# Branch C's output projection as seven block products in a hybrid encoder trunk

## The chip, the cores and the metric

The kernel runs on one core of a Trainium2 chip. The metric is the device time of one execution in microseconds. Engines are named as the profile names them: PE (matmuls) with PEld (its weight loads), DVE and ACT (vector and scalar work), POOL, and SP, which only issues DMAs here. L12 is line 12 of the kernel before.

## The reference

Two layers of an encoder trunk over 512 positions of 1024 channels, all in float32. Per layer:

```python
xn = rms_norm(x, ln1[l])
z = xn @ w_in[l]                       # all branches' columns and the gates gz
y_a = rms_norm(o_a, a_norm[l]) * silu(a_g)         # o_a: gated linear scans, 4 heads
y_b = spatial_gating(gelu(b_u), gelu(b_v), w_s[l], b_s[l])
y_c = window_attention(qh, kh, vh, sink[l])        # 512 x 512
gates = sigmoid(gz.reshape(bsz, s_len, 3, D_MODEL))
merged = (gates[:, :, 0] * (y_a @ w_br[l, 0])
          + gates[:, :, 1] * (y_b @ w_br[l, 1])
          + gates[:, :, 2] * (y_c @ w_br[l, 2]))   # each w_br: 512 x 1024
x = x + merged @ w_out[l]
hn = rms_norm(x, ln2[l])
x = x + square(relu(hn @ w_up[l])) @ w_down[l]
```

A final rms_norm follows. The change touches the last term of `merged`, a product of 512 x 512 by 512 x 1024 in each layer, and the place of some norm work at the start of layer 0.

## The kernel before, in words

**Precision and matmul form.** Every float32 operand of a large product is split into a high and a low part (fp32r): ACT casts the high part, DVE subtracts it from the original to get the low part (`split`, L255, for activations; `wsplit`, L201, for weights, 128 x 1024 at a time). A product of two such pairs takes three matmuls: high by high, low by high, high by low. A weight chunk is loaded by SP (512 KB) into one of two buffers `wr` (`wload`, L179); its parts lie in one of three buffers `wh` and `wl`.

**Block products.** Several large products already go through `seven` (L422). A product is cut into 2 x 2 blocks on each side and computed as seven block products in place of eight, from sums of blocks: `left_sums` (L375) makes the sums of the left operand (differences of 256 columns, then splits of 512), and in `seven` DVE adds the weight blocks in place before products 6, 5 and 4. The order of products is 1, 2, 6, 7, 5, 4, 3. Products 1, 6, 5 and 3 accumulate in the same two PSUM banks, and so do 7 and 4, so each result is read out by a callback `on` before the next product of that chain adds to it: P1, P2 (added to P1's result), P16, P7, P165, P74, P1653. Weight splits, weight sums and callbacks are traced with raised priority (`hp`, L124).

**Order of the work.** The program is traced in Python and a scheduler puts each engine's instructions into an order by priority, against its own model of time; on the chip each engine runs its queue in that order. `later(n)` lowers the priority of what it holds, `behind(mark)` binds instructions of one engine behind another instruction.

**Layer, stage by stage.** From the norm (`n1`: split tiles `xs` in 16 slots with the tag "x") come first three units of `seven`, u = 0 to 2, K = 1024 (24 matmuls for each block product): u = 0 the values of branches A and B (`on_tok`), u = 1 and 2 the gates of branches C and A (`on_gate`), which are passed through tanh and written to DRAM (`thd`). In layer 0 the norm's reciprocal root `rc` is late, so `on_tok` works unscaled. After product 7 of unit 0 comes `norm_rows` (L347): four matmuls against the identity (eight in the trace) spread `rc` over rows (`bc`, L285), ACT copies them to `rb`. After the unit, L896 to L898 scale the eight tiles vt and bv by `rc` on ACT. DVE's three small scalings of `rc` (L835 to L837) stand ahead of unit 0.

Then heads of branch A's scan (`a_head`, L617), branch B, branch C's attention (`c_run`, L1096) and projections are traced with priorities that let them interleave. Branch C's output comes as four tiles `yc`, 128 features by 512 positions each; the last, yc[3], comes from the transposes at L1067, the products `po` at L1078 and a copy at L1080. At L1125 the output gates of branch A (`gate_a`, four projections `ag`) are traced, and behind them **branch C's projection**, L1128 to L1137: the four yc are split, and for each half fl of the 1024 output channels `proj_tok` (L236) runs two weight chunks of two k-tiles each, for four blocks of 128 positions, into four PSUM banks (m, m, c, c). DVE multiplies each bank by its gate plus one (L1136) into `mC`, eight tiles in the slots "x". The gates come back from DRAM by POOL (`gates`, L1082) into seven slots "ch". Branch A's gates (`tha`) are loaded into "x" as well. Branch A's projection `yA` follows (L1165), is gated (L1168) and added (L1169), the sum is transposed (`mT`, L1153), and `wo` follows.

Of the kernel before, what the change touches and what calls it, by code (L numbers as in the profile page):

```python
# [6 lines left out]
F32 = mybir.dt.float32  # L7
# [5 lines left out]
P = 128  # L13
# [46 lines left out]
def trunk(tc, xT, xt, ws, vec, fnb, bsb, snk, wst, rope, cmask, amask, ident, out):  # L60
# [26 lines left out]
    part = {}  # L87
    BANKS = {"m": 2, "a": 2, "c": 2, "s": 2}
    PAIRS, AHEAD = ((), (2,), (2,), (2,)), ((), (1,), (1,), (1,))
    GROUPS = (("m", "m", "c", "c"), ("a", "a", "s", "s"))  # L90
    WR, WB, NZ, NSM, NQ = 2, 3, 2, 3, 8

# [254 lines left out]
    def norm_rows(n):  # L347

        pt = bcast(n.rc)
        n.rb = T("rb", "rb")  # L350
        nc.scalar.copy(n.rb, pt)
# [20 lines left out]
        h.update({2: two(v_, 0), 4: two(v_, 1)})  # L372
        return left_sums(new, h, u, v, sb_, held)

    def left_sums(new, h, u, v, sb_=None, held=False):  # L375
        V = nc.vector
        a11, a21, a12, a22 = u[:, 0:HT], u[:, HT:], v[:, 0:HT], v[:, HT:]
        if sb_ is None:
            sb_ = part["wq"].tile([P, 2, HT], F32, tag="sf", bufs=2, name=nm("sf"))
            V.tensor_tensor(sb_[:, 0], a11, a21, ALU.subtract)  # L380
        sa = part["wq"].tile([P, 2, HT], F32, tag="sf", bufs=2, name=nm("sf"))
        V.tensor_tensor(sa[:, 0], a22, a21, ALU.subtract)
        V.scalar_tensor_tensor(sa[:, 1], sa[:, 0], -1.0, a11, ALU.mult, ALU.subtract)
# [12 lines left out]
        if not held:  # L396
            first(new)
        V.scalar_tensor_tensor(sb_[:, 1], a12, -1.0, sa[:, 1], ALU.mult, ALU.subtract)
        if held:
            return first, second  # L400
        second(new)
# [20 lines left out]
    def seven(raw, hs, name, on, order=(1, 2, 6, 7, 5, 4, 3), between=None, after=1, apart=False, swap=False):  # L422

        b11, t3, b22, b21 = raw
        V = nc.vector

        banks = {}
        use = {1: ("c", b11, "P1"), 2: ("m", b21, "P2"), 6: ("c", b11, "P16"), 7: ("a", t3, "P7"),
               5: ("c", t3, "P165"), 4: ("a", b21, "P74"), 3: ("c", b22, "P1653")}

        def mms(pt, p, k, xh, xl, hi, lo, c, start):
            t = slice(p * P, (p + 1) * P)
            nc.tensor.matmul(pt, xh[:, t], hi[:, c], start=start and k == 0, stop=False, skip_group_check=True)  # L433
            nc.tensor.matmul(pt, xl[:, t], hi[:, c], start=False, stop=False, skip_group_check=True)  # L434
            nc.tensor.matmul(pt, xh[:, t], lo[:, c], start=False, stop=k == 3, skip_group_check=True)  # L435

        for n in order:
            tag, w, which = use[n]
            bank = {"c": "a", "a": "c"}.get(tag, tag) if swap else tag
            start = n in (1, 2, 7)  # L440
            if start:
                banks[tag] = [PT(bank, name + {"c": "A", "m": "B", "a": "C"}[tag]) for _ in range(2)]
            pts = banks[tag]
            with hp():
                for i in range(2):
                    if n == 6:
                        V.tensor_tensor(b11[i], b11[i], t3[i], ALU.add)
                    elif n == 5:
                        V.tensor_tensor(t3[i], b11[i], b22[i], ALU.subtract)
# [3 lines left out]
            for s_ in range(2):  # L453
                with hp():
                    split_w.append(wsplit(w[s_]))
                if not apart or n != order[-1]:
                    for k2 in range(2):
                        c = slice(k2 * S, (k2 + 1) * S)
                        for p in range(2):
                            mms(pts[p], p, 2 * s_ + k2, *hs[2 * s_ + k2][n], *split_w[s_], c, start)  # L460
# [325 lines left out]
    for l in range(DEPTH):  # L786
# [25 lines left out]
        def project_bu():  # L812
            pts = proj_four(xs, "bu", l, "bu", banks="mmcc" if l else "mmaa")
            if l == 0:
                raw = [T("l2", "bu") for _ in pts]
                for t, pt in zip(raw, pts):
                    nc.scalar.copy(t, pt)
                return raw
            norm_rows(n1)
            return [evac(pt, "l2", "bu") for pt in pts]  # L820
# [40 lines left out]
                bv[p] = T("tv", "bv")  # L861
                A.activation(bv[p], pt, AF.Copy, scale=nlo)

        past = []

        def on_gate(i):
            w = {}

            def keep(z, t, fl):
                nc.gpsimd.dma_start(thd[:, i * 4 + t, fl * S:(fl + 1) * S], z)  # L870

            def on(which, p, pt):
                A, V = nc.scalar, nc.vector
                if which in ("P1", "P16", "P7"):
                    w[which, p] = T("zt", "zt")
                    A.copy(w[which, p], pt)
# [12 lines left out]
        for u in range(3):  # L889
            nxt = uload(l, "un", u + 1) if u < 2 else None  # L890
            if u == 0:
                if l:
                    seven(raw, hx, "t", on_tok, (1, 7, 6, 2, 5, 4, 3), lambda: bu.extend(project_bu()), swap=(u + l) % 2)
                else:
                    seven(raw, hx, "t", on_tok, (1, 2, 6, 7, 5, 4, 3), lambda: norm_rows(n1), 7, swap=(u + l) % 2)
                    for t in vt + bv:  # L896
                        i = (vt + bv).index(t) % 4
                        nc.scalar.activation(t, t, AF.Copy, scale=rc[:, i:i + 1])  # L898
# [339 lines left out]
        for qd in range(4):  # L1238
# [30 lines left out]
                    if f == 3:  # L1269
                        early_sums(raw, mark)  # L1270

            def between():
# [141 lines left out]
```

## Time and profile before

| | us |
|---|---|
| median of 3 runs (1647.73 to 1648.71) | 1648.09 |
| profiled execution | 1647.19 |
| its span, first to last instruction | 1645.4 |
| branch C's projection, layer 0: first and last matmul start | 392.93 and 426.26 |
| the same, layer 1, last | 1243.3 |

The profile is of one execution. A row of a timeline has the start in us, the duration, engine, line, operation, output and inputs with their shapes; in brackets stands how long the engine was idle before it and what ended that. Matmuls are pipelined: a 512-column matmul is shown with 0.39 us, while the next one starts earlier. A row of the groups has the count, the busy time, the mean in ns and the idle time before. A row of stretches has the length and the busy time of each engine in that stretch.

### The profile page before, as it was taken

The numbers are of one execution on the slowest core, as the hardware profiler recorded it, in microseconds if no ns is written. First come the engines' busy times: TensorE is split into PE (matmuls) and PEld (weight loads), VectorE is DVE, ScalarE is ACT, GpSimd is POOL, SyncE is SP. The second block draws the span as 40 slices with busy tenths as digits, with TensorE's granted clock in tenths as the row PEclk, the third lists the DMA queues.
The fourth block names the chain that finished last, engine by engine and source line by source line (L and its number), as shares of the span: only waits on it lengthen the run. The fifth ranks groups of instructions, "written<-read, shape, count | busy, mean of one in ns | idle before, by whom it ended". The sixth has DMA issues, their size and how long they took to land.

```text
span 1645.4 us, 24316 instructions
## 1 busy us (share of the span) xinstructions
PE 1631.2 (99%) x9137; PEld 1376.4 (84%) x9137; DVE 1359.1 (83%) x2183; ACT 1013.8 (62%) x1731; POOL 102.9 (6%) x165
## 2 busy tenths in 40 slices
PE   9999999999999999999999999999999999999997
PEld 7788888888888898989888888888888888989896
DVE  7888979677758988888989869887877589898987
ACT  7667567677247564646666655886862464647374
POOL 0012000000300000000010110000003000000001
PEclk9999999999999999999999999999999999999999
DMA  8343221322625233232423432222226343232411
GB/s 309 103 153 125 77 90 72 103 97 84 237 90 192 99 107 103 103 107 98 141 90 125 145 121 77 77 84 103 97 78 243 108 162 119 87 128 77 129 65 52
DMA packets 55590, 191.55 MB, mean 116 GB/s; under 512 B 7376, under 2 KB 7632, under 8 KB 55472
## 3 DMA queue, kind: packets, MB, share of 16 engines
q1 hardware_dynamic: 44352, 154.43, 27.4%
q0 software_dynamic: 10688, 35.00, 5.7%
q8 instruction: 72, 1.18, 0.3%
q10 hardware_dynamic: 432, 0.55, 0.1%
q14 instruction: 46, 0.38, 0.1%
HBM read 173.18 MB, written 16.78 MB: 115 GB/s over the span
## 4 chain that ended last, share of the span: by engine, by line
PE 91%; ACT 3%; DVE 3%; DMA 2%; issue 1%; POOL 0%; SPq 0%; POOLq 0%; DVEq 0%; ACTq 0%
PE up L208 4%; PE up L209 4%; PE up L210 4%; PE dA L434 4%; PE dA L433 4%; PE dA L435 4%; PE us L522 2%; PE us L524 2%; PE us L523 2%; PE f L210 2%; PE f L209 2%; PE wo L252 2%; PE wo L250 2%; PE f L208 2%; PE wo L251 2%; PE dC L434 2%
## 5 line engine op out<-in xcount | busy, mean ns | idle before, releaser
L203 ACT CAST wh<-wq 128x1024 fp32r<-128x1024 f32 x214 | 225.3, 1053 | 206.2 <-PE dA L434 56.4
L204 DVE TENSOR_TENSOR wl<-wq,wh 128x1024 fp32r<-128x1024 f32 x214 | 259.9, 1219 | 66.5 <-ACT wh L203 64.4
L203 ACT CAST wh<-wr 128x1024 fp32r<-128x1024 f32 x164 | 172.0, 1049 | 156.4 <-PE wo L251 27.1
L204 DVE TENSOR_TENSOR wl<-wr,wh 128x1024 fp32r<-128x1024 f32 x164 | 199.9, 1219 | 62.3 <-ACT wh L203 56.1
L210 PE MATMUL up<-xh,wl 128*128 128x512 f32 x320 | 124.7, 390 | 0.0
L209 PE MATMUL up<-xl,wh 128*128 128x512 f32 x320 | 124.7, 390 | 0.0
L208 PE MATMUL up<-xh,wh 128*128 128x512 f32 x320 | 124.4, 391 | 0.0
L434 PE MATMUL dA<-wh,sh 128*128 128x512 f32 x256 | 99.7, 389 | 0.0
L433 PE MATMUL dA<-wh,sh 128*128 128x512 f32 x256 | 98.4, 389 | 0.0
L435 PE MATMUL dA<-wl,sh 128*128 128x512 f32 x256 | 91.8, 389 | 0.0
L656 DVE TENSOR_TENSOR ex<-ex 128x512 f32<-128x512 f32 x112 | 74.8, 685 | 3.4 <-ACT kt L647 3.2
L210 PEld LDWEIGHTS up<-xh,wl 128*128 128x128 f32 x320 | 60.1, 188 | 12.4
L208 PEld LDWEIGHTS up<-xh,wh 128*128 128x128 f32 x320 | 60.1, 188 | 12.2
L209 PEld LDWEIGHTS up<-xl,wh 128*128 128x128 f32 x320 | 60.1, 188 | 12.2
L644 ACT ACTIVATE qt<-ex 128x512 f32<-128x512 f32 x56 | 37.9, 677 | 31.4 <-DVE ex L656 29.8
L435 PEld LDWEIGHTS dA<-wl,sh 128*128 128x128 f32 x256 | 48.1, 188 | 10.0
L433 PEld LDWEIGHTS dA<-wh,sh 128*128 128x128 f32 x256 | 48.0, 188 | 10.0
L434 PEld LDWEIGHTS dA<-wh,sh 128*128 128x128 f32 x256 | 48.0, 188 | 9.9
L523 PE MATMUL us<-xs,wh 128*128 128x256 f32 x192 | 54.0, 283 | 0.0
L522 PE MATMUL us<-xs,wh 128*128 128x256 f32 x192 | 54.0, 283 | 0.0
L524 PE MATMUL us<-xs,wl 128*128 128x256 f32 x192 | 53.3, 283 | 0.0
L208 PE MATMUL gz<-xh,wh 128*128 128x512 f32 x128 | 51.0, 399 | 0.7 <-DVE gz L792 0.7
(438 smaller groups left out, 4775.7 us busy)
## 6 DMA issues: line engine op xcount, KB each, us to landing
wr<-in_ws_dram SPq DMA_DIRECT2D x158, 512.0 KB, 3.5
wq<-in_ws_dram SPq DMA_DIRECT2D x124, 512.0 KB, 4.3
thd<-zt POOLq DMA_DIRECT2D x32, 256.0 KB, 2.6
gt<-thd POOLq DMA_DIRECT2D x32, 256.0 KB, 4.3
mgd<-mg POOLq DMA_DIRECT2D x16, 256.0 KB, 2.6
mB<-mgd POOLq DMA_DIRECT2D x16, 256.0 KB, 6.6
x<-in_xT_dram SPq DMA_DIRECT2D x8, 256.0 KB, 7.7
xt<-in_xt_dram SPq DMA_DIRECT2D x8, 256.0 KB, 7.9
```

Of the source, the lines that this page charges most:

```text
L203: nc.scalar.copy(hi, raw)
L204: nc.vector.tensor_tensor(lo, raw, hi.bitcast(F32), ALU.subtract)
L208: nc.tensor.matmul(pt, whi, xhi, start=first, stop=False)
L209: nc.tensor.matmul(pt, whi, xlo, start=False, stop=False)
L210: nc.tensor.matmul(pt, wlo, xhi, start=False, stop=last)
L433: nc.tensor.matmul(pt, xh[:, t], hi[:, c], start=start and k == 0, stop=False, skip_group_check=True)
L434: nc.tensor.matmul(pt, xl[:, t], hi[:, c], start=False, stop=False, skip_group_check=True)
L435: nc.tensor.matmul(pt, xh[:, t], lo[:, c], start=False, stop=k == 3, skip_group_check=True)
L522: nc.tensor.matmul(pt, hi[:, c], xh, start=n in (1, 2, 7) and k == 0, stop=False, skip_group_check=True)
L523: nc.tensor.matmul(pt, hi[:, c], xl, start=False, stop=False, skip_group_check=True)
L524: nc.tensor.matmul(pt, lo[:, c], xh, start=False, stop=k == 3, skip_group_check=True)
L656: nc.vector.tensor_tensor(o_ap, o_ap, ap_of(ex, i_, [[istep, 2]] + z), ALU.add)
```

## The change

Branch C's projection goes through `seven`. Four weight chunks are loaded at once, the first two into the `wr` buffers, the others into two buffers of the tag "z2". The left blocks are made from yc[k] and yc[k + 2], k = 0 and 1, by `left_sums`, whose temporaries and sums now lie in the slots "x". Product 1 needs yc[0] and yc[1], product 2 needs yc[2] and yc[3], the other five need sums of all four. Each product has 12 matmuls. Products 7 and 4 use the banks "s" (which the attention uses too), the others c and m. `on_yc` evicts P1, P16, P7 and P1653 on ACT, adds the others on DVE from PSUM into the same tiles, and gates each finished tile on DVE. The eight gates of branch C are asked for in the order in which the tiles are finished.

In layer 0 the norm broadcast moves from behind product 7 of unit 0 to behind product 1 of unit 1, and the eight scalings to behind the first ACT copy of unit 1.

`seven` becomes general in the number of weight tiles and k-tiles, takes the bank map as an argument, and hands its `between` the last matmul of the first product; for the other users this leaves the work as it was. The diff without those lines:

```diff
-    def left_sums(new, h, u, v, sb_=None, held=False):
+    def left_sums(new, h, u, v, sb_=None, held=False, sf=None):
...
-        sa = part["wq"].tile([P, 2, HT], F32, tag="sf", bufs=2, name=nm("sf"))
+        sa = sf() if sf else part["wq"].tile([P, 2, HT], F32, tag="sf", bufs=2, name=nm("sf"))
...
-            if n == after and between:
-                between()
+            if n == order[0] and between:
+                between(end_)
...
+        def rows_behind(mark):
+            with behind(mark):
+                norm_rows(n1)
+
-        past = []
+        past, kept = [], []
...
-                    A.copy(w[which, p], pt)
+                    kept.append(A.copy(w[which, p], pt))
...
-                    seven(raw, hx, "t", on_tok, (1, 2, 6, 7, 5, 4, 3), lambda: norm_rows(n1), 7, swap=(u + l) % 2)
-                    for t in vt + bv:
-                        i = (vt + bv).index(t) % 4
-                        nc.scalar.activation(t, t, AF.Copy, scale=rc[:, i:i + 1])
+                    seven(raw, hx, "t", on_tok, (1, 2, 6, 7, 5, 4, 3), swap=TURN if (u + l) % 2 else None)
             else:
-                seven(raw, hx, "g", on_gate(u - 1), swap=(u + l) % 2)
+                seven(raw, hx, "g", on_gate(u - 1), between=None if l or u > 1 else rows_behind, swap=TURN if (u + l) % 2 else None)
+                if l == 0 and u == 1:
+                    with behind(kept[0]):
+                        for ts in (vt, bv):
+                            for i, t in enumerate(ts):
+                                nc.scalar.activation(t, t, AF.Copy, scale=rc[:, i:i + 1])
...
-            ys = y_split(yc, "yh")
-            mcs = []
-            for fl in range(2):
-                th = gates("ch", 0, fl)
-                pts = proj_tok(ys, "yC", (l, "y", 2, fl), 0)
-                mcs.append([T("x", "mC") for _ in range(4)])
-                for t in range(4):
-                    with hp():
-                        nc.vector.scalar_tensor_tensor(mcs[fl][t], th[t], 1.0, pts[t], ALU.add, ALU.mult)
+            raw = []
+            for i, (kh, fl) in enumerate(((0, 0), (0, 1), (1, 1), (1, 0))):
+                with hp():
+                    t = Z2("wb").rearrange("p a b -> p (a b)") if i > 1 else sb.tile([P, CW], F32, tag="wr", bufs=WR, name=nm("wr"))
+                    nc.sync.dma_start(t, ws[CHUNK[(l, "y", 2, fl, kh)]])
+                raw.append([t])
+            early_sums(raw)
+            hy = []
+            for k in range(2):
+                u, v = yc[k], yc[k + 2]
+                p1 = T("yh", "yh", F32R).rearrange("p (a b) -> p a b", a=2)
+                split(u[:, 0:HT], p1[:, 0], p1[:, 1])
+                v_ = (T("yh", "yh", F32R), T("yh", "yl", F32R))
+                split(v, *v_)
+                h = {1: (p1[:, 0], p1[:, 1]), 2: two(v_, 0), 4: two(v_, 1)}
+                left_sums(lambda: T("x", "ysum", F32R), h, u, v, sf=lambda: T("x", "sf").rearrange("p (a b) -> p a b", a=2))
+                hy.append(h)
+            mcs = [[None] * 4, [None] * 4]
+            th = {}
+            for fl, t in ((0, 0), (0, 1), (1, 2), (1, 3), (0, 2), (0, 3), (1, 0), (1, 1)):
+                th[fl, t] = T("ch", "gt")
+                nc.gpsimd.dma_start(th[fl, t], thd[:, t, fl * S:(fl + 1) * S])
+
+            def on_yc(which, p, pt):
+                A, V = nc.scalar, nc.vector
+                t, fl = {"P1": (p, 0), "P2": (p, 0), "P16": (2 + p, 0), "P74": (2 + p, 0), "P7": (2 + p, 1), "P165": (2 + p, 1), "P1653": (p, 1)}[which]
+                if which in ("P1", "P16", "P7", "P1653"):
+                    mcs[fl][t] = T("x", "mC")
+                    A.activation(mcs[fl][t], pt, AF.Copy, scale=-1.0 if fl else 1.0)
+                else:
+                    V.tensor_tensor(mcs[fl][t], mcs[fl][t], pt, ALU.subtract if fl else ALU.add)
+                if which in ("P2", "P165", "P74", "P1653"):
+                    V.scalar_tensor_tensor(mcs[fl][t], th[fl, t], 1.0, mcs[fl][t], ALU.add, ALU.mult)
+
+            seven(raw, hy, "v", on_yc, swap={"a": "s"})
```

More of the change, by code (lines that the diff above doesn't have):

```diff
@@ L89, in trunk @@
     PAIRS, AHEAD = ((), (2,), (2,), (2,)), ((), (1,), (1,), (1,))
+    TURN = {"c": "a", "a": "c"}
     GROUPS = (("m", "m", "c", "c"), ("a", "a", "s", "s"))
@@ L378, in left_sums @@
         if sb_ is None:
-            sb_ = part["wq"].tile([P, 2, HT], F32, tag="sf", bufs=2, name=nm("sf"))
+            sb_ = sf() if sf else part["wq"].tile([P, 2, HT], F32, tag="sf", bufs=2, name=nm("sf"))
             V.tensor_tensor(sb_[:, 0], a11, a21, ALU.subtract)
-        sa = part["wq"].tile([P, 2, HT], F32, tag="sf", bufs=2, name=nm("sf"))
+        sa = sf() if sf else part["wq"].tile([P, 2, HT], F32, tag="sf", bufs=2, name=nm("sf"))
         V.tensor_tensor(sa[:, 0], a22, a21, ALU.subtract)
@@ L420, in early_sums, with seven @@
                 nc.vector.tensor_tensor(b12, b12, b22, ALU.add)
-    def seven(raw, hs, name, on, order=(1, 2, 6, 7, 5, 4, 3), between=None, after=1, apart=False, swap=False):
+    def seven(raw, hs, name, on, order=(1, 2, 6, 7, 5, 4, 3), between=None, apart=False, swap=False):
         b11, t3, b22, b21 = raw
@@ L434, in mms @@
             nc.tensor.matmul(pt, xl[:, t], hi[:, c], start=False, stop=False, skip_group_check=True)
-            nc.tensor.matmul(pt, xh[:, t], lo[:, c], start=False, stop=k == 3, skip_group_check=True)
+            return nc.tensor.matmul(pt, xh[:, t], lo[:, c], start=False, stop=k == len(hs) - 1, skip_group_check=True)
         for n in order:
             tag, w, which = use[n]
-            bank = {"c": "a", "a": "c"}.get(tag, tag) if swap else tag
+            bank = swap.get(tag, tag) if swap else tag
             start = n in (1, 2, 7)
@@ L444, in seven @@
             with hp():
-                for i in range(2):
+                for i in range(len(b11)):
                     if n == 6:
@@ L452, in seven @@
             split_w = []
-            for s_ in range(2):
+            for s_ in range(len(w)):
                 with hp():
@@ L459, in seven @@
                         for p in range(2):
-                            mms(pts[p], p, 2 * s_ + k2, *hs[2 * s_ + k2][n], *split_w[s_], c, start)
+                            end_ = mms(pts[p], p, 2 * s_ + k2, *hs[2 * s_ + k2][n], *split_w[s_], c, start)
             for p in range(2):
@@ L892, in trunk @@
                 if l:
-                    seven(raw, hx, "t", on_tok, (1, 7, 6, 2, 5, 4, 3), lambda: bu.extend(project_bu()), swap=(u + l) % 2)
+                    seven(raw, hx, "t", on_tok, (1, 7, 6, 2, 5, 4, 3), lambda mark: bu.extend(project_bu()), swap=TURN if (u + l) % 2 else None)
                 else:
-                    seven(raw, hx, "t", on_tok, (1, 2, 6, 7, 5, 4, 3), lambda: norm_rows(n1), 7, swap=(u + l) % 2)
-                    for t in vt + bv:
-                        i = (vt + bv).index(t) % 4
-                        nc.scalar.activation(t, t, AF.Copy, scale=rc[:, i:i + 1])
-            else:
-                seven(raw, hx, "g", on_gate(u - 1), swap=(u + l) % 2)
+                    seven(raw, hx, "t", on_tok, (1, 2, 6, 7, 5, 4, 3), swap=TURN if (u + l) % 2 else None)
+            else:
+                seven(raw, hx, "g", on_gate(u - 1), between=None if l or u > 1 else rows_behind, swap=TURN if (u + l) % 2 else None)
[4 more added lines that the diff above has]
+                                nc.scalar.activation(t, t, AF.Copy, scale=rc[:, i:i + 1])
             if nxt:
@@ L1270, in trunk, with between @@
                         early_sums(raw, mark)
-            def between():
+            def between(mark):
                 for part_ in rest:
```

## The prediction

> **What bounds the kernel now.** I read the page first (busy shares, then the chain that ended last), then a table of stretches around branch C's projection in both layers, then the timeline of each engine there, and last the first 100 us for the moved norm steps.
>
> ```profile
> PE 1631.2 (99%) x9137; PEld 1376.4 (84%) x9137; DVE 1359.1 (83%) x2183; ACT 1013.8 (62%) x1731; POOL 102.9 (6%) x165
> PE 91%; ACT 3%; DVE 3%; DMA 2%; issue 1%; POOL 0%; SPq 0%; POOLq 0%; DVEq 0%; ACTq 0%
> PE bc L285 <- POOL rs L278: 1.0, 1, 1.0
> ```
>
> The busy shares, the chain and a line of PE's waits (total, times, longest) say one thing: the program is a string of matmuls, and the wait of the norm broadcast that this change moves is one of the few that interrupt it. A matmul taken off this string is worth its start-to-start time, not its shown duration, so I take the pitch from the timeline (start, duration), first and fifteenth of a run:
>
> ```profile
> 392.70 0.39 PE L210 MATMUL ag<-xh,wl 128*128 128x512 f32 x1
> 392.93 0.39 PE L250 MATMUL yC<-wh,yh 128*128 128x512 f32 x1
> ...
> 396.10 0.39 PE L252 MATMUL yC<-wl,yh 128*128 128x512 f32 x1
> ```
>
> Fourteen pitches in 396.10 - 392.93 = 3.17 us: 0.2264 us each. But PE being full says nothing of what happens when the other engines get more to do. This is the stage, layer 0 then layer 1 (columns: length, then busy time and count of PE, PEld, DVE, ACT, POOL, then granted clock, DMA share, GB/s):
>
> ```profile
> 387.00:399.00 12.00, 12.00 (x116) 9.86 (x114) 11.88 (x28) 10.45 (x26) 0.00 (x0) 1.00 0.30 100
> 399.00:411.00 12.00, 11.66 (x101) 10.09 (x100) 4.08 (x9) 5.20 (x11) 0.55 (x1) 1.00 0.22 73
> 411.00:427.00 16.00, 16.00 (x75) 13.20 (x74) 10.82 (x17) 5.51 (x13) 4.87 (x9) 1.00 0.39 132
> 427.00:447.00 20.00, 20.00 (x94) 16.51 (x93) 12.50 (x17) 4.37 (x5) 9.03 (x17) 1.00 0.93 353
> 1217.00:1229.00 12.00, 11.81 (x104) 10.34 (x104) 4.09 (x9) 6.70 (x19) 0.54 (x1) 1.00 0.24 84
> 1229.00:1245.00 16.00, 16.00 (x74) 13.23 (x73) 11.75 (x18) 4.77 (x9) 5.34 (x9) 1.00 0.42 141
> 1245.00:1265.00 20.00, 20.00 (x94) 16.46 (x93) 11.88 (x17) 4.45 (x6) 8.55 (x16) 1.00 0.95 352
> ```
>
> DVE is full until 399 (the last scan head and the softmax), a third busy to 411, two thirds busy to 427. Layer 1 repeats it.
>
> **Part one: matmuls removed.** Each layer's projection has 2 halves x 4 k-tiles x 4 token blocks x 3 = 96 matmuls; seven products of 2 k-tiles x 2 blocks x 3 make 84. Twenty-four go in all: 24 x 0.2264 = 5.4 us off the string. [...]
>
> **Part two: what DVE and ACT get instead.** The prices (line, engine, shapes, count, busy us and mean ns):
>
> ```profile
> L204 DVE TENSOR_TENSOR wl<-wr,wh 128x1024 fp32r<-128x1024 f32 x164 | 199.9, 1219 | 62.3 <-ACT wh L203 56.1 <-PE xT L330 5.8
> L203 ACT CAST wh<-wr 128x1024 fp32r<-128x1024 f32 x164 | 172.0, 1049 | 156.4 <-PE wo L251 27.1 <-PE f L209 19.9 <-PE yA L251 19.9
> L258 ACT CAST sh<-sf 128x512 fp32r<-128x512 f32 x64 | 39.4, 615 | 3.3 <-DVE sf L383 2.9 <-DVE sf L398 0.3
> ```
>
> A queued DVE instruction starts a little before the one ahead of it ends:
>
> ```profile
> 41.39 0.68 DVE L849 SCALAR_TENSOR_TENSOR vt<-tB,vt 128x512 f32<-128x512 f32 x1
> 41.99 0.41 DVE L382 TENSOR_TENSOR sf<-x,x 128x256 f32<-128x256 f32 x1
> 42.32 0.68 DVE L849 SCALAR_TENSOR_TENSOR vt<-tB,vt 128x512 f32<-128x512 f32 x1
> ...
> 44.46 1.22 DVE L449 TENSOR_TENSOR wq<-wq,wq 128x1024 f32<-128x1024 f32 x1
> 45.60 1.22 DVE L204 TENSOR_TENSOR wl<-wq,wh 128x1024 fp32r<-128x1024 f32 x1
> ```
>
> So 1.14, 0.60 and 0.33 us of DVE per 1024, 512 and 256 columns. Per layer the change adds at 1024 columns three low halves of weights (7 products against 4 chunks) and four weight sums (one early, one each for products 6, 5, 4): 7 x 1.14 = 8.0. At 512: low halves 6 against 4, eight gatings as before, and six new accumulations of a product into its result, 8 x 0.60 = 4.8. At 256: two low halves of the first quarter and eight left sums, 10 x 0.33 = 3.3. Sum 16.1 us of DVE per layer. ACT gets three more weight casts, two more left casts and eight evictions of 512, two casts of 256: at most 3 x 1.05 + 10 x 0.62 + 2 x 0.4 = 10.2 us; it idles 6.8 + 10.5 = 17.3 us between 399 and 427, so ACT costs nothing unless a cast stands behind a wait.
>
> DVE is the tight one. Idle from 399 to 427: 7.9 + 5.2 = 13.1 us; layer 1: 7.9 + 4.2 = 12.2. The stretch is to shrink by the 2.7 us saved, which leaves 10.4 and 9.5 for 16.1: 5.7 to 6.6 us do not fit. Of that 3.6 (the last two accumulations and four gatings, 6 x 0.60) may follow the last product, into a stretch with 7.5 and 8.1 us idle. What must fit and does not is 2.1 + 3.0 = 5.1 us in both layers together. That is one end; the other is nothing, since weight splits run ahead of PE and some of the new work can be done before 399. I take the middle, 2.5 us, because of the next point.
>
> **The late quarter.** Branch C's last quarter of features, yc[3], ends late (start, duration):
>
> ```profile
> 397.84 0.51 ACT L1055 ACTIVATE sc<-sc,es 128x256 f32<-128x256 f32 x1
> 402.68 0.60 PE L1067 MATMUL pT<-id_t,sc 128*128 128x128 f32 x4
> 404.89 1.97 PE L1078 MATMUL po<-sc,cvt 128*64 128x128 f32 x32
> 408.58 0.59 ACT L1080 COPY yc<-po 128x512 f32<-128x512 f32 x1 [3.33 <-PE po L1078]
> 408.88 0.49 PE L728 MATMUL av<-st,qd 128*128 128x128 f32 x2 [0.34 <-DVE st L712]
> ...
> 410.91 1.17 PE L250 MATMUL yC<-wh,yh 128*128 128x512 f32 x4
> ```
>
> Before, three of four k-tiles of the first half, 36 matmuls or 8.2 us, fill PE until then. After, only product 1 and half of product 2 need no yc[3]: 18 matmuls, 4.1 us (the sums of tiles 0 and 2 sit in the slots of x, free when the last gate matmul at 392.70 is done, and DVE has no room for them until 399). The rest of PE's queue moves up by up to 4.1 us. It can: the last softmax piece is ready at 398.35, its transposes start at 402.68, 4.3 us of slack. What eats it is new weight work ahead of it on the full DVE: product 6's weights have raised priority and need the early sum and one add, 2.3 us; PE may then idle about 2 us per layer. This and the DVE overflow overlap, hence the middle.
>
> Other queues. The page's row of weight loads (count, size, median us to landing), then POOL and a gating on DVE:
>
> ```profile
> wr<-in_ws_dram SPq DMA_DIRECT2D x158, 512.0 KB, 3.5
> 408.85 0.55 POOL L1087 DMA_DIRECT2D gt<-thd  x1 [22.37 <-PE po L1078]
> 431.00 1.43 DVE L1168 SCALAR_TENSOR_TENSOR gt<-gt,yA 128x512 f32<-128x512 f32 x2 [2.48 <-DMA gt<-thd]
> ```
>
> SP's loads are as many as before, but the two wr buffers stay held through products 5 and 4, so branch A's first weights load later: they land in 3.5 us, and products 5, 4 and 3 are 36 matmuls, 8.2 us, of cover. On POOL the gates are asked for in a new order; POOL already waits 22 us for a gate buffer, and branch A's gatings 2.5 us for their gates, while PE stays full; a little more or less is hidden by branch A's second half (48 matmuls, 10.9 us). Nothing, from both sides.
>
> **Part three: broadcast and scalings moved.**
>
> ```profile
> 44.63 4.03 POOL L278 TENSOR_TENSOR rs<-ms,mhalf_t 128x4 f32<-128x4 f32 x1 [14.10 <-DVE ms L276]
> 48.71 1.16 PE L285 MATMUL bc<-id_t,rs 128*128 128x128 f32 x8 [1.05 <-POOL rs L278]
> 51.53 0.73 PE L433 MATMUL tC<-wh,xs 128*128 128x512 f32 x2 [0.28 <-ACT xs L258]
> 52.88 0.50 PE L434 MATMUL tC<-wh,xs 128*128 128x512 f32 x1 [0.61 <-DVE xs L259]
> 48.69 1.34 ACT L898 ACTIVATE vt<-vt,rs 128x512 f32<-128x512 f32 x2 [3.56 <-POOL rs L278]
> 75.17 0.59 ACT L876 COPY zt<-gA 128x512 f32<-128x512 f32 x1 [1.21 <-PE gA L435]
> 75.00:90.00 15.00, 15.00 (x68) 12.43 (x67) 11.35 (x11) 9.19 (x12) 1.15 (x2) 1.00 0.30 103
> ```
>
> PE waits 1.05 us for the reciprocal root, then 0.28 and 0.61 for a split that stood on ACT behind a scaling waiting 3.56 us for the same root. All three, 1.94 us, have that cause. The eight matmuls and the copy are only moved. DVE's small scalings of the root still wait for it in place, so a split on DVE can still come late: between 1.0 and 1.9 us gained, I take 1.5. The eight scalings (two take 1.34 us, so 5.4) land on ACT after 75.17, where 5.8 of 15 us are idle: no cost; a cast behind one of them would be 0.7 us late, under a product of 24 matmuls (5.4 us).
>
> **Sum.** -5.4 - 1.5 + 2.5 = -4.4 us. The profiled execution took 1647.19 (span 1645.4 and 1.8 around it) and would take 1642.8; it lies 0.9 below the median of 1648.09, so on the median I expect 1643.7. The bounds of the terms give -5.4 - 1.9 + 0 = -7.3 (1640.8) to -5.4 - 1.0 + 5.1 = -1.3 (1646.8). About 0.2%, 3.3 us, is what a measurement of this kernel can tell from no change: faster is below 1644.8, slower above 1651.4.
>
> **Rivals.** First, the cover moves and nothing is won: yc[3] stays at 408.58 because its chain on the full DVE slips as far as PE runs ahead. Before, 60 matmuls follow it, after, 66: 6 x 0.2264 = 1.4 us later per layer, +2.7 - 1.5 = +1.2, 1649.3. For it: DVE at 11.88 of 12 us ahead. Against: the 4.3 us of slack.
>
> Second, slower: the left sums of yc[3] on DVE become the bound. They are not raised in priority, while weight sums, low halves, accumulations and gatings are. From yc[3] to product 6's second half stand 0.41 + 0.41 + 0.62 + 0.68 = 2.1 us; product 2's four accumulations and gatings (2.4), one weight sum and one low half (2.3) put in front make it 6.8. PE has the scan head's products (408.88 to 410.91, 2.0) and half of product 2 (1.4) meanwhile, so it idles 3.4 us, on top of the 1.4 of the first rival: 4.8 per layer, +9.6 - 1.5 = +8.1, 1656.2. It turns slower when both layers lose 2.4 us each, that is once about 2.3 us of DVE work slips in front of the sums. Against it: with three buffers of split weights these run up to two products ahead of PE, so little of that work need fall just there. [...]
>
> Third, the moved broadcast does not do what it is for: the split waits on DVE behind the root's scalings instead of on ACT, and nothing of the 1.94 us comes back while the scalings push a cast. Then -5.4 + 2.5 = -2.9, 1645.2, within 0.2%.
>
> **Chances.** The forecast 0.62, of which 0.53 lies below 1644.8 and 0.09 in the upper end of its terms; the first rival 0.22, the third 0.04, the slower one 0.12. Faster 0.53, within 0.2% 0.35, slower 0.12. The range runs from 1640.5, just under the forecast's low bound, to 1649.5, just over the first rival; what it leaves out is the slower rival and some 0.05 beside. Within its own case the forecast runs from 1640.8 to 1646.8.
>
> **What would show it.** Right: 168 matmuls of the projection; no wait of bc on the root, the tC waits gone by 55 us; DVE over 80% busy in the twelve us after its full stretch; yc[3] 2 to 4 us earlier relative to the last gate matmul; PE waits on left splits or wl of 1 to 2 us per layer. Wrong: PE idle for over 2.4 us per layer before product 6 or 7, on a low half; or no idle time at all, which puts the time at the low bound; or PE waiting for branch A's weights or gates, which I priced at nothing.

## The result, and the profile after

After the change the kernel takes 1661.69 us (median; 1661.29 to 1662.36), against 1648.16 before on the same chip: ratio 1.0085, 95% interval 1.0073 to 1.0097. It is slower by 13.5 us, where 1643.7 was forecast and 1649.5 was the top of the range. One of the twelve runs of e11 below took 2323 us at a granted clock of 0.65; its ratio leaves that run out, and without it its median is 1644.89. The profiled execution took 1662.36, its span is 1660.6.

The page (busy shares, then the chain that ended last), and PE's longest waits (total, times, longest):

```profile
PE 1632.9 (98%) x9113; PEld 1378.2 (83%) x9113; DVE 1390.5 (84%) x2233; ACT 1032.5 (62%) x1761; POOL 102.3 (6%) x165
PE 87%; DVE 8%; ACT 3%; issue 1%; POOL 0%; DMA 0%; POOLq 0%; DVEq 0%; ACTq 0%
```

```profile
PE pT L1074 <- DVE sc L1060: 7.0, 2, 6.8
PE kT L702 <- ACT at L686: 3.7, 2, 3.4
PE vC L434 <- ACT ysum L259: 1.9, 1, 1.9
```

The 24 matmuls are gone (9113 instead of 9137), yet PE is busy 1.7 us longer. At the pitch of 0.2264 us they were worth 5.4 us, so the rest of the work takes 7.1 us more: a lower clock (0.993 on average, 0.999 before; its stretches are in the last section). PE's time without work (span less busy) grew from 14.2 to 27.7 us. DVE has risen from 3% to 8% of the chain.

Five of the stretches of the prediction (length, then busy time of PE, PEld, DVE, ACT and POOL, then granted clock):

```profile
387.00:399.00 12.00, 10.91 (x82) 8.92 (x83) 12.00 (x24) 10.88 (x26) 0.00 (x0) 1.00 0.00 0
399.00:411.00 12.00, 8.03 (x45) 7.22 (x45) 7.40 (x18) 4.04 (x12) 0.00 (x0) 0.72 0.14 45
411.00:427.00 16.00, 13.27 (x81) 10.06 (x78) 11.52 (x19) 9.50 (x22) 4.32 (x7) 0.89 0.41 132
...
1217.00:1229.00 12.00, 5.92 (x56) 4.52 (x54) 12.00 (x25) 9.36 (x20) 0.00 (x0) 0.87 0.06 21
1229.00:1245.00 16.00, 13.98 (x131) 11.98 (x132) 10.67 (x26) 9.90 (x31) 0.54 (x1) 0.88 0.15 50
```

PE lacks 7.8 us in the first three rows and 8.1 in the last two, where before it lacked 0.3 and 0.2. That is 15.4 us more idle time, all of the growth of 13.5 and the 1.9 us that the moved broadcast gave back, and it lies in the two stages that the projection was changed in. Positions say the same: from the first matmul of the last gate projection to the last of branch A's, layer 0 took 85.83 us before and takes 96.19, layer 1 86.69 and 94.07. Each should have become 2.7 us shorter.

The loss does not lie behind yc[3], where the prediction looked, but ahead of it. Here is layer 1, PE and DVE by start and duration:

```profile
1222.69 0.39 PE L436 MATMUL vB<-wl,yh 128*128 128x512 f32 x1
1229.86 1.51 PE L1074 MATMUL pT<-id_t,sc 128*128 128x128 f32 x6 [6.78 <-DVE sc L1060]
```

```profile
1221.81 0.42 DVE L399 SCALAR_TENSOR_TENSOR sf<-yc,sf 128x256 f32<-128x256 f32 x1
1222.14 1.22 DVE L205 TENSOR_TENSOR wl<-wr,wh 128x1024 fp32r<-128x1024 f32 x1
...
1223.34 0.69 DVE L260 TENSOR_TENSOR ysum<-sf,ysum 128x512 fp32r<-128x512 f32 x1
...
1226.76 0.16 DVE L1057 RECIPROCAL es<-es 128x2 f32<-128x2 f32 x1
1226.83 1.21 DVE L205 TENSOR_TENSOR wl<-wr,wh 128x1024 fp32r<-128x1024 f32 x1
1227.95 0.69 DVE L260 TENSOR_TENSOR ysum<-sf,ysum 128x512 fp32r<-128x512 f32 x1
1228.55 0.42 DVE L381 TENSOR_TENSOR sf<-yc 128x256 f32<-128x256 f32 x1
...
1229.29 0.42 DVE L1060 TENSOR_SCALAR sc<-sc,es 128x384 f32<-128x384 f32 x1
```

PE's queue has come to the transposes of a softmax piece, one of those that yc[3] is made from, and stops there. Its reciprocal is ready at 1226.92; its scaling, 0.4 us of work, comes at 1229.29, because a low half of weights, a low half of a left sum and a left sum (L205, L260, L381) are queued between the two on DVE, with small work of the scan head. In layer 0 PE's long wait is one step away, at the transposes of the last scan head (`kT`), which wait through ACT's copy for a masked copy on the same DVE queue (`own`, L635):

```profile
402.99 0.64 PE L702 MATMUL kT<-id_t,kd 128*128 128x128 f32 x3 [3.35 <-ACT at L686]
401.88 0.36 ACT L686 COPY at<-at 64x256 f32<-64x256 f32 x1 [2.20 <-DVE own L635]
404.68 0.51 ACT L1062 ACTIVATE sc<-sc,es 128x256 f32<-128x256 f32 x1 [0.48 <-DVE es L1057]
```

The last softmax piece is late there too: it is scaled on ACT at 404.68 instead of 397.84, and yc[3] is copied at 413.16 instead of 408.58, although PE arrived 1.7 us earlier.

How much stands ahead shows in one stretch per layer, from the first matmul of the last gate projection to the last `po` matmul. Before, then after (the last row ends 0.3 us too early; to the end of that `po`, at 1240.55, DVE's figure is 45.61):

```profile
362.18:408.54 46.36, 46.36 (x393) 38.52 (x391) 39.28 (x90) 34.62 (x79) 1.71 (x3) 1.00 0.28 98
1178.39:1226.02 47.63, 47.44 (x402) 39.52 (x400) 37.93 (x90) 35.83 (x87) 2.18 (x3) 1.00 0.24 84
```

```profile
360.44:413.11 52.67, 47.60 (x394) 40.16 (x391) 45.98 (x102) 36.51 (x89) 2.50 (x4) 0.94 0.17 56
1186.92:1240.24 53.32, 45.22 (x382) 37.42 (x381) 45.34 (x100) 37.84 (x90) 2.18 (x3) 0.94 0.14 45
```

DVE (third figure) does 6.7 and 7.7 us more before yc[3] exists, 12 and 11 instructions more.

Part three did what was forecast. PE no longer waits for the broadcast (a wait of 0.87 us on a split of weights on DVE has come up at 50.65), and the scalings (the first four and four, 0.65 us each) run on ACT beside a full PE:

```profile
72.99 1.05 PE L286 MATMUL bc<-id_t,rs 128*128 128x128 f32 x8
72.99 2.56 ACT L907 ACTIVATE vt<-vt,rs 128x512 f32<-128x512 f32 x4
```

The first matmul of `f` starts at 145.15 instead of 146.88, and the gain holds until layer 0's last gate projection.

### The profile page after: what moved, and what is told of

Read it like the earlier page. It is cut to its first block, busy times and chain, and to the rows that moved or that the text cites. A ratio compares the mean times of both kernels' runs of the same rounds, so it can differ in the third digit from the quotient of the medians.

```text
span 1660.6 us, 24370 instructions
## 1 busy us (share of the span) xinstructions
PE 1632.9 (98%) x9113; PEld 1378.2 (83%) x9113; DVE 1390.5 (84%) x2233; ACT 1032.5 (62%) x1761; POOL 102.3 (6%) x165
## 4 chain that ended last, share of the span: by engine, by line
PE 87%; DVE 8%; ACT 3%; issue 1%; POOL 0%; DMA 0%; POOLq 0%; DVEq 0%; ACTq 0%
PE up L209 4%; PE up L210 4%; PE up L211 4%; PE dA L435 3%; PE dA L436 3%; PE dA L434 3%; PE us L523 2%; PE us L525 2%; PE us L524 2%; PE f L211 2%; PE f L210 2%; PE f L209 2%; PE wo L253 2%; PE wo L252 2%; PE wo L251 2%; PE dC L435 2%
## 5 line engine op out<-in xcount | busy, mean ns | idle before, releaser
L205 DVE TENSOR_TENSOR wl<-wq,wh 128x1024 fp32r<-128x1024 f32 x214 | 260.3, 1220 | 66.3 <-ACT wh L204 64.5
L205 DVE TENSOR_TENSOR wl<-wr,wh 128x1024 fp32r<-128x1024 f32 x164 | 200.2, 1221 | 49.3 <-ACT wh L204 42.2
```

The source lines that it names most:

```text
L205: nc.vector.tensor_tensor(lo, raw, hi.bitcast(F32), ALU.subtract)
```

## The experiments

My theory after reading the trace: the loss is the new DVE work that stands ahead of yc[3] (**queue**). Rivals: it is the shorter cover, 18 matmuls instead of 36 (**cover**); it is the amount of DVE work, wherever it stands (**load**); or it is the new dependences of the sums (**chain**). Ratios are to the kernel before, with 95% intervals.

| run | median us | ratio |
|---|---|---|
| after | 1661.69 | 1.0085 [1.0073, 1.0097] |
| e1_norm_only | 1646.17 | 0.9992 [0.9983, 1.0000] |
| e2_dve_load | 1661.94 | 1.0090 [1.0074, 1.0105] |
| e3_cover | 1652.06 | 1.0031 [1.0019, 1.0042] |
| e4_not_raised | 1661.61 | 1.0087 [1.0073, 1.0101] |
| e5_pool_sums | 1668.03 | 1.0125 [1.0110, 1.0140] |
| e6_held_back | 1653.60 | 1.0040 [1.0025, 1.0055] |
| e7_load_behind | 1652.28 | 1.0030 [1.0018, 1.0041] |
| e8_no_sums | 1646.00 | 0.9988 [0.9980, 0.9997] |
| e9_gating_late | 1649.46 | 1.0013 [1.0004, 1.0021] |
| e10_dma_sums | 1649.14 | 1.0010 [1.0002, 1.0019] |
| e11_both | 1645.10 | 0.9984 [0.9975, 0.9993] |
| e12_unbound | 1648.99 | 1.0009 [1.0000, 1.0018] |

**e1_norm_only**: the kernel before with part three alone.

> The kernel before with part three alone: the norm broadcast and the eight scalings moved, the projection as it was. In the changed kernel all matmuls from unit 1 to the last gate projection of layer 0 stand 1.7 us earlier than before, so every theory of the loss in the projection expects about -1.7 us here (1646.4 on a median of 1648.1). If it shows no gain, the moved norm work also costs something later that the shifted times hide.

-1.4 us, with an interval that reaches no change. Part three is worth what it was priced at, and the whole loss is the projection's: against this run the kernel after is 15.5 us slower.

**e2_dve_load**: the kernel before, with two idle DVE instructions (a maximum of a tile with itself) on each of the projection's four weight chunks.

```diff
             nc.sync.dma_start(raw, ws[CHUNK[key]])
+            for _ in range(extra):          # 2 for the chunks of yC
+                nc.vector.tensor_tensor(raw, raw, raw, ALU.max)
             return wsplit(raw)
```

> The kernel before, with two idle DVE operations of 1024 columns (a weight chunk's maximum with itself, same values) ahead of the split of each of branch C's four weight chunks: 8 x 1.14 = 9.1 us of DVE per layer, of which three chunks' share, 6.8 us, stands ahead of yc[3]; matmuls and their cover unchanged. Queue theory (the loss is new DVE work queued on the full DVE ahead of the last scan head and attention block): 6.8 less the 4.3 us of slack, 2.5 us per layer, about +5 (1653). Cover theory (the loss is that 18 matmuls fill PE where 36 did): no change, within 1 us. Chain theory (the loss is the split and sum chain behind yc[3]): no change, within 1 us.

+14.4 us, all of the change's loss, with neither a block product nor a shorter cover. The idle instructions as a group in layer 0 (count, busy us, mean ns), and the waits that they made:

```profile
L186 DVE TENSOR_TENSOR wr<-wr 128x1024 f32<-128x1024 f32 x8 | 9.7, 1216 | 0.0
```

```profile
PE pT L1069 <- DVE es L1051: 4.4, 1, 4.4
PE at L630 <- ACT wh L205: 3.1, 1, 3.1
```

PE stops in the same stage, in layer 1 in front of the softmax transposes, in layer 0 in front of the scan head's products (`at`). I had expected +5, with three quarters of them ahead of yc[3]; in the trace all sixteen stand ahead of it. At 1.14 us from start to start they are 18.2 us in both layers, and each us cost 0.8.

**e3_cover**: the kernel before, with the chunk that holds yc[2] and yc[3] taken first, so that yc[3] is needed after 12 matmuls instead of 36.

```diff
-            hi, lo = wload(*key, i)
+            j = nk // 2 - 1 - i if turn else i     # turn for yC
+            hi, lo = wload(*key, j)
```

> The kernel before, with branch C's two weight chunks of each half taken in the other order, so that yc[3] is needed after 12 matmuls of the projection, not after 36: 24 matmuls or 5.4 us of cover fewer per layer, DVE and ACT work unchanged. Cover theory: the missing cover is lost in full, +10.9 (1659). Queue theory: 5.4 less the 4.3 us of slack, 1.1 us per layer, +2 (1650). Chain theory: no change.

+4.5 us for a cover shorter than the change's. It counts, but it is a third of the loss at most.

**e4_not_raised**: the kernel after, with the seven products of branch C not raised in priority.

```diff
-            with hp():
+            with up():       # nullcontext for branch C's products
```

> The changed kernel with one thing undone: in this use of the seven products weight sums, weight splits, accumulations and gatings are not raised in priority, so that the scheduler puts the last scan head and the attention ahead of them on DVE. Queue theory: most of the 8 us of new DVE work moves behind yc[3], PE idles 0 to 2 us per layer ahead of it, and the time falls to 1641 to 1648. Chain theory: the work behind yc[3] only grows, 1661 or more. Cover theory: the cover is as small as in the changed kernel, 1660 to 1662.

Nothing changed: every engine's instructions came out in the same order as in the kernel after. My premise was false. The order is not set by the raising. My reading is that the planner puts work that is ready into what its own model takes for gaps, while on the chip DVE has none there; no run shows the planner's model.

**e5_pool_sums**: the kernel after, with the four weight sums per layer on POOL.

```diff
-        V = nc.vector
+        V = sums or nc.vector       # nc.gpsimd for branch C's products
```

> The changed kernel with the four weight sums of each layer's projection on POOL, not on DVE: 4 x 1.14 = 4.6 us less DVE work per layer, nearly all of which the changed kernel's trace shows ahead of yc[3]. Queue theory, as it stands after the first runs (each us of DVE work that the scheduler puts into the full stretch ahead of yc[3] is lost nearly in full): about 2 x 4.6 = 9 us come back, 1652, unless POOL's sums, whose price no row shows, come later than the products need them. Chain theory (the loss is behind yc[3]): 1657 to 1662, since only product 4's sum stands there.

Slower by another 6 us. The timeline shows why (POOL's sums and the DVE instructions that start beside them):

```profile
385.88 2.38 POOL L448 TENSOR_TENSOR wr<-wr,wr 128x1024 f32<-128x1024 f32 x1 [1.07 <-DVE wl L205]
385.99 2.81 DVE L993 SCALAR_TENSOR_TENSOR ag<-th,ag 128x512 f32<-128x512 f32 x1
...
393.95 2.47 POOL L452 TENSOR_TENSOR wb<-wb,wr 128x1024 f32<-128x1024 f32 x1 [5.70 <-issue]
...
394.16 2.54 DVE L383 TENSOR_TENSOR sf<-yc,yc 128x256 f32<-128x256 f32 x1
```

The two DVE instructions, of 0.68 and 0.41 us elsewhere, start beside a POOL sum and last until 0.54 and 0.28 us after that has ended. Each of these two sums takes 2.1 us of DVE to save 1.14.

**e6_held_back**: the kernel after, with the new DVE work bound behind the last softmax scaling and the last product of the scan head: early sum, left sums, weight sums, and the low halves of the weights of all products but 1 and 2.

```diff
+            def held():
+                with behind(marks["c"]), behind(tail[0]):
+                    yield
...
-            early_sums(raw)
+            with held():
+                early_sums(raw)
```

> The changed kernel with the new DVE work (early sum, left sums and their low halves, weight sums, and the weight low halves of all products but 1 and 2) bound in DVE's queue behind the last softmax scaling of the attention and the last product of scan head 3's state queries, which PE's transposes and products wait for. No work is taken away. Queue theory: yc[3] comes as early as in the kernel before or earlier, the clock stays at full, and the time falls to 1642 to 1648; what is left is waits behind yc[3]. Load theory (16 us more DVE work per layer cost the same wherever they stand, as the stage is bound by DVE): 1657 or more.

8 us come back, which is less than the queue theory's range and more than the load theory's. The last `po` matmul of layer 0 ends at 401.0, 7.5 us earlier than before the change (2.7 of it are there already at the first matmul of the last gate projection); the place of the work was the cause of this part. The kernel is still 7.4 us slower than e1, and that is now lost behind yc[3], where the same work meets branch A's gatings and the merged sum:

```profile
PE stp L709 <- ACT kd L706: 3.0, 2, 2.5
PE mT L1196 <- DVE gt L1211: 2.3, 4, 1.4
...
PE mT L1196 <- DVE mC L1212: 1.2, 4, 0.5
```

**e7_load_behind**: the kernel before, with six idle DVE instructions per layer, bound behind the low half of yc[3].

```diff
+            if key in extra:
+                with behind(extra[key]):
+                    for _ in range(3):
+                        nc.vector.tensor_tensor(raw, raw, raw, ALU.max)
```

> The kernel before with six idle DVE operations of 1024 columns per layer (6.8 us, as much as stood ahead of yc[3] in the kernel with eight), all bound behind the low half of yc[3] in DVE's queue: three on the projection's last weight chunk, three on branch A's first. Queue theory: they fall into idle DVE time, 0 to +2 us (1648 to 1650). Load theory: six eighths of the +14.4 us of the kernel with eight, about +11 (1659).

+4.8 us for 13.7 us of work: 0.35 us per us behind yc[3], against 0.8 ahead of it. Neither queue alone (0 to 2) nor load alone (11) holds; work costs time in both stretches, and more in the first.

**e8_no_sums**: the kernel after, without the weight sums and left sums (with their low halves) of branch C's projection: products 3 to 7 multiply unsummed tiles. PE does the same 84 matmuls per layer.

> The kernel after, with the four weight sums and the left sums (eight sums and four low halves) of branch C's projection left out in each layer, so that products 3 to 7 multiply unsummed weights and unsummed left sides: the same 84 matmuls per layer, 9.6 us less DVE work per layer (4 x 1.14 + 8 x 0.33 + 4 x 0.60), and so 6.5 of the 16.1 new us left. Load theory (DVE work ahead of and around yc[3] is the whole loss): after lost 20.4 us against its ideal of 1641.3 for 32.2 us of new work, so 13.0 us left of it lose 8 in proportion and less if a threshold is passed: 1643 to 1650. Rival, the cover (18 matmuls instead of 36 between the last gate projection and the first use of yc[3] starve PE whatever DVE does): still 1655 or more, since the cover stays as short.

1646.0, within the load theory's interval, where the cover's was 1655 or more: with 9.6 us of the 16.1 per layer gone, the projection is no longer slower than before. By itself the run does not part the rivals. In its trace 24 matmuls of the projection, not 18, precede the last `po`, and with the sums their casts on ACT and the waits for them are gone too. What rules out those rivals is e2, which has the loss without a sum or a shorter cover, and e11 below, which has the 18 matmuls and all the sums without the loss.

**e9_gating_late**, **e10_dma_sums** and **e11_both** build on e6. The first binds six of branch C's gatings behind branch A's last low half; the second lets DMAs make the weight sums; the third does both.

```diff
-                if which in ("P2", "P165", "P74", "P1653"):
+                if which == "P2":
...
+        with behind(cut):        # the low half of branch A's last head
+            for fl, t in sorted(late_):
+                nc.vector.scalar_tensor_tensor(mcs[fl][t], th[fl, t], 1.0, mcs[fl][t], ALU.add, ALU.mult)
```

```diff
+            add = lambda o, i_: nc.gpsimd.dma_start(o, i_, accum_op=ALU.add)
...
+                    if n == 6:
+                        add(w11, w12)
+                    elif n == 5:
+                        nc.sync.dma_start(w12, src(0, 1))
+                        add(w12, src(0, 0))
+                    elif n == 4:
+                        add(w21, w11)
...
+                add(w12, src(1, 1))
```

> e6_held_back, with six of the eight gatings of branch C's products (those of products 5, 4 and 3) bound behind the low half of branch A's last scan head. e6 lost 4.9 and 4.1 us per layer in the turn of the merged sum, where branch A's last low half came at 428.18 instead of 424.38. Queue theory (those gatings stand in front of branch A's chain): 2 to 4 us per layer come back, 1646 to 1650. Rival (the load behind yc[3] is what it is; moving 6 x 0.68 us by some places only moves the wait to yA's first gatings): 1652 to 1655.

> e6_held_back, with the four weight sums per layer made by DMAs that add into the tile (issued by POOL, the fourth chunk's second load by SP) instead of four 1.14 us DVE instructions: 4.6 us less DVE work per layer, nothing computed on POOL. Load theory: e6 stands 12.3 us over the ideal with some 16 us of new work per layer; 4.6 us less per layer gives 3 to 7 us back, 1646.5 to 1650.5. Rival (the adding DMAs come late, in POOL's queue behind the gate loads, and products 6, 5 and 4 wait for their weights; or POOL's descriptors block DVE as its sums did in e5): 1654 or more, with PE waits at vA and vC that end on weight splits.

> e9 and e10 together: the gatings of products 5, 4 and 3 bound behind branch A's last low half, and the weight sums made by DMAs. Load theory: if both pay, 1642 to 1648, and it may pass e1 (1646.2). Rival (each only moves the wait): 1651 or more.

By the medians 4.1 and 4.5 us come back, and 8.5 with both: the two add up. e11 is faster than both kernels, 16.6 us below the one after and 0.9984 of the one before. PE's longest waits in it:

```profile
PE idle L168 <- DVE idle L165: 1.6, 1, 1.6
PE tA L436 <- DVE wl L205: 1.3, 1, 1.3
PE yA L251 <- ACT mC L1189: 1.1, 1, 1.1
PE po L1090 <- ACT sc L1080: 1.1, 2, 0.6
```

No wait on DVE of more than 0.3 us is left in the two stages. DVE's work ahead of yc[3] (third figure) is near that of before in layer 0, 39.46 us to the end of the last `po` at 401.82 (the first row stops short of it) against 39.28, and is 2.9 us more in layer 1:

```profile
360.62:400.19 39.57, 39.05 (x338) 32.51 (x338) 39.05 (x91) 32.81 (x77) 4.39 (x6) 1.00 0.46 119
1174.43:1219.56 45.13, 43.98 (x382) 36.08 (x380) 40.79 (x97) 37.06 (x90) 4.84 (x6) 1.00 0.40 100
```

PE's busy time is 1626.5 us, 4.7 less than before, at a clock of 0.998 on average and 1.00 in both rows. From the first matmul of the last gate projection to the last of branch A's, layer 0 takes 83.35 us, 2.5 of the 2.7 forecast; layer 1 takes 87.57, 0.9 more than before. Of the 3.6 us that layer 1 still loses, 2.3 are waits of PE that end on ACT: 1.15 us on the softmax and its copies ahead of yc[3], and 1.11 on an eviction of `mC` at the start of `yA`. The rest I have not settled. e11 against e1 is -0.0008 in the ratios, within their intervals; that the projection pays by itself rests on layer 0's positions.

**e12_unbound**: e11 without the binding.

```diff
             def held():
-                with behind(marks["c"]), behind(tail[0]):
-                    yield
+                yield
```

> e11_both without the binding: the weight sums are still made by DMAs and the gatings of products 5, 4 and 3 still wait for branch A's last low half, but nothing is held behind the softmax of yc[3]; some 4 to 5 us per layer of DVE work (left sums of yc[0] and yc[2] with their low halves, low halves of weights) then stands ahead of yc[3] again. Place theory (what stands ahead of yc[3] on the full DVE costs 0.8 us for each us, by the 18.2 us of e2 that cost 14.4): 6 to 8 us slower than e11, 1650 to 1654. Rival, amount theory (only the amount of DVE work counts, wherever it stands): as e11, 1643.5 to 1647.

3.9 us slower than e11, with the same instructions: place counts by itself, though for less than the 6 to 8 us that I forecast. PE waits again where it waited after the change:

```profile
PE pT L1079 <- DVE sc L1065: 3.4, 3, 1.6
```

## Why the prediction was wrong

**The step that failed** is the one under "The late quarter": "What eats it is new weight work ahead of it on the full DVE: product 6's weights have raised priority and need the early sum and one add, 2.3 us". The mechanism was right, the size was not: by the trace 6.7 and 7.7 us more stand there, since all four weight sums, the left sums of yc[0] and yc[2] with their low halves and the low halves of the weights come ahead, and not product 6's alone. Two reasons behind it fell. The order does not follow the raised priority (e4). And the full DVE (12.00 us busy of the 12 from 387) kept no work away: the prediction said of the left sums that their slots are free only after the last gate matmul and that "DVE has no room for them until 399", but in the trace their first difference runs at 387.79, ahead of the last gate matmul at 390.86. The work put ahead of yc[3], 6.7 and 7.7 us, pushed the whole chain back by nearly its own length (the stretch to the last `po` grew by 6.3 and 6.0 us); 4.3 us of slack cannot hold 7.

In the sum the step is the term of +2.5 us. Against e1 the change cost 15.5 us, and 5.4 us of matmuls were saved beside it, so by these figures the term was some 21.

**Part one**: 24 matmuls at 0.2264 us, 5.4 us. Nearly right: in e11 PE's busy time is 4.7 us below that of before and 4.1 below that of e1, and layer 0 is 2.5 us shorter of 2.7. After the change the gain is there, and buried.

**Part two's amount**, 16.1 us of DVE per layer, is borne out: the page's DVE time grew by 31.4 us for both layers. The price that I put on it was not. I counted only what did not fit between 399 and 427 (5.1 us) and took half. That sum asks whether a stretch can hold the work, not who waits meanwhile. Measured with nothing else changed, a us of DVE work cost 0.8 ahead of yc[3] (e2) and 0.35 behind it (e7).

**yc[3]** was to come 2 to 4 us earlier against the last gate matmul. It came 6.4 us later in layer 0 (21.86 us from the one to the last `po` matmul, before 15.45) and 7.9 in layer 1.

**The first rival**, cover without gain, is a part of it: e3 gives 4.5 us for a cover even shorter, but e11 keeps the 18 matmuls and is not slower than before. **The slower rival** had DVE as the bound and work slipping in front of a chain, and missed the place: after yc[3] PE waits 1.9 us on a left sum once, ahead of it 6.8 and 3.4. It also left out the clock: 1.00 in every stretch that the prediction shows of the kernel before, and 0.72 from 399 to 411 after the change.

**Part three**: forecast 1.5, measured 1.4 (e1) and 1.73 by position. **SP and POOL**, priced at nothing: right, no long wait of PE ends on a load. **ACT**, at nothing "unless a cast stands behind a wait": the 1.9 us wait ends on ACT's cast of a left sum, with a weight cast ahead of it that had itself waited 1.0 us.

## What to carry to other kernels

Trading matmuls for vector work lost here where it landed ahead of a chain on a full vector engine (1.0085 after the change), and no longer once its place and amount were changed (0.9984 in e11): price the added work by its place in the queue ahead of the chain that PE will wait for next, not by whether the stage's idle time can hold it. A scheduler may put ready work ahead of urgent work, as it did here; bind such work behind the last instruction of the urgent chain (8 us here, and 3.9 in e12 for leaving it out), and let DMAs make sums of weights where they have room (4.5 us here; the DMA share in e11's two stretches is 0.46 and 0.40). When a change like this loses, load the old kernel with idle instructions ahead of and behind the chain: two runs give the price of each place.

## What the hardware showed

**After three waits of PE the clock was at half.** One-us stretches of the kernel after, in layer 0 (PE's last matmul before its 3.35 us wait ends at 399.64) and layer 1 (its wait goes from 1223.08 to 1229.86); the clock is the figure after POOL's count:

```profile
402.00:403.00 1.00, 0.01 (x1) 0.02 (x1) 1.00 (x3) 0.96 (x4) 0.00 (x0) 1.00 0.07 16
403.00:404.00 1.00, 0.63 (x3) 0.29 (x3) 1.00 (x3) 0.64 (x2) 0.00 (x0) 0.66 0.00 0
...
409.00:410.00 1.00, 1.00 (x7) 1.00 (x7) 0.00 (x0) 0.00 (x0) 0.00 (x0) 0.50 0.00 0
410.00:411.00 1.00, 1.00 (x12) 0.88 (x13) 0.00 (x0) 0.18 (x2) 0.00 (x0) 0.93 0.00 0
...
1225.00:1226.00 1.00, 0.00 (x0) 0.00 (x0) 1.00 (x3) 0.92 (x4) 0.00 (x0) 0.96 0.00 0
1226.00:1227.00 1.00, 0.00 (x0) 0.00 (x0) 1.00 (x4) 0.90 (x4) 0.00 (x0) 0.50 0.00 0
...
1231.00:1232.00 1.00, 1.00 (x16) 0.70 (x15) 1.00 (x2) 1.00 (x4) 0.00 (x0) 0.50 0.06 16
1232.00:1233.00 1.00, 1.00 (x24) 0.95 (x22) 1.00 (x3) 1.00 (x5) 0.00 (x0) 0.62 0.00 0
```

By these figures the clock was at half from 403.3 to 410.1: it fell 3.7 us after that matmul's end, with the wait of 3.35 us between them, and rose after some 7 us of work. At 0.50 the 512-column matmuls start 0.43 us apart (2.56 us for six, from 420.72 to 423.28), against 0.2264 at 1.00, so PE runs at about half speed there: for the over 6 us of its work from 403.3 to 410.1 that is, by an estimate from these times, about 3 us lost. In layer 1 the clock fell 2.8 us after the start of idleness and rose after 2.9 us of work, an estimated 1.5 us. The third fall, from 420.4 to 423.8 (the clock is 0.69 from 420 to 421, 0.50 to 423, and 0.60 to 424), cost an estimated 1.7; ahead of it PE had waited only 1.95 us and worked on both sides of the wait. Together they are some 6 of the 7.1 us that PE's work took longer. How long a wait brings the clock down is not shown: these three falls give no single length.

**Beside POOL's sums DVE took longer**: 2.81 us for an instruction of 0.68, and 2.54 for one of 0.41 (e5). The DMAs that add, issued by POOL too, showed no such thing: in e11's stage of layer 0 every 512-column group of DVE stays at 0.67 to 0.70 us on average, and by the rows of issues in e11 their 512 KB land in 4.4 to 5.5 us (median), against 3.5 for a plain load.

```profile
wr<-in_ws_dram SPq DMA_DIRECT2D x156, 512.0 KB, 3.5
wr<-in_ws_dram POOLq DMA_DIRECT2D x4, 512.0 KB, 5.5
wb<-wr POOLq DMA_DIRECT2D x2, 512.0 KB, 4.4
```
